# k k^T and k q^T of the delta rule as one three-part product, contiguous blocks from the transposes, and a remade table of issue

## The chip, the cores and the metric

One NeuronCore of a Trainium2 chip runs the whole program. The metric is the device time of one execution in microseconds (us), lower is better. In the profile PE is TensorE's matrix multiply and PEld its loading of weights, DVE is VectorE, ACT ScalarE, POOL GpSimd, and SP the engine that issues most DMAs.

## The reference

The model is an encoder of two layers over 512 positions of width 1024. Each layer projects its normalized input into three branches, gMLP, retention and a gated delta rule (here GDN), merges them with gates, and adds the result to its input. The change lies in the delta rule, which runs in both directions over chunks of 64 positions:

```python
def gdn_direction(q, k, v, beta, g):
    ...
    decay = jnp.exp(jnp.where(incl, gc[..., :, None] - gc[..., None, :], -jnp.inf))
    kb = kc * bc[..., None]
    lower = jnp.where(strict, jnp.einsum("nbhid,nbhjd->nbhij", kb, kc) * decay, 0.0)
    eye = jnp.eye(c, dtype=F32)
    rhs = jnp.concatenate([vc * bc[..., None], kb * jnp.exp(gc)[..., None]], axis=-1)
    sol = lax.linalg.triangular_solve(lower + eye, rhs, left_side=True, lower=True)
    u, w = sol[..., :GDN_HD], sol[..., GDN_HD:]

    def step(state, inp):
        qi, ki, ui, wi, gi, di = inp
        v_new = ui - jnp.einsum("bhcd,bhde->bhce", wi, state)
        scores = jnp.einsum("bhqd,bhkd->bhqk", qi, ki) * di
        out = (jnp.einsum("bhcd,bhde->bhce", qi * jnp.exp(gi)[..., None], state)
               + jnp.einsum("bhqk,bhke->bhqe", scores, v_new))
        ...
```

So per head and chunk k k^T and k q^T are needed, then the inverse of a lower triangular matrix.

## The kernel before

**Dense products.** All large products go through `mm3` (L279 to L283): each operand is split into a high part of type fp32r and the rest, and three products (high by high, high by low, low by high) add up in PSUM, each 128 rows, 128 columns of weights and 512 moving columns. The weights come by DMA from SP; ACT casts the high part (`hi`, L273) and DVE subtracts (`lo`, L274). PE runs such products through nearly the whole program, and DVE's L274 feeds it.

**The delta rule.** `gdn_pair(pi)` (L686) does two heads, `m` = 0 and 1; there are two pairs per layer, four in the program. It uses chunks of 128 positions, four per head. Its steps:

- L698 to L715: the dense products for k, q and v (`dpg`), a short convolution and SiLU on DVE and ACT, which give `kT` and `qT` (L684), and transposes on PE (`ptgg`, L706).
- L741 to L747: per head four products k k^T (`kkg`, L743) and four k q^T (`qkg`, L746) of 128x128 in plain fp32, each kind in a PSUM bank of its own out of the two of tag `gd`. PE takes a plain fp32 product as two records in the trace.
- L748 to L765: the decay factors `ef`, `eb`, `el` (L752, L754), and the products with them: `sl` (L757, L759) from k k^T, `pf` (L763) and `pb` (L765) from k q^T.
- L774 to L793: the inverse. DVE transposes blocks of 32x32 out of `sl` into `zn` (L774), runs 31 elimination steps over all blocks at once (L787, L789, result in `zv`), and transposes `zv` in two ways, into `ov` (L792, in the place of `zn`) and `ou` (L793). In both results the index of the matrix stands innermost, so one 32x32 block is read at a stride of 32 elements.
- L796 to L807: the blocks are joined. `px` (L799) has 32 products with `ov` as the moving operand, `xs` takes the result times -1 (L801 on ACT, L802 on DVE), and `py` (L806) has 32 products with `ou` as weights; all have 32 columns. The two halves `b` use the lower and the upper 64 rows.
- L809 to L865: copies into `sec` and `sl` (L816 to L818), two larger joins of the same kind with 64 columns (`pw`, L834; `pz`, L841 and L844), and scaling.
- L878 to L927: four steps of the scan in each direction.

**What sets the order.** At the end `in_order` (L139) ties the instructions of every engine into the order of the table `ORDER` (L26), a list of jumps and run lengths per engine: between the small steps of the delta rule PE has dense products of other branches. In pair 0 these are the gates and outputs of the retention branch (`merge(1, ...)`, tiles `pg` and `pb`), in pair 1 the gMLP branch and `merge(0, ...)`. An engine works its own list in order, and waits where an operand is not ready.

Of the kernel before, what the change touches and what calls it, by code (L numbers as in the profile page):

```python
# [8 lines left out]
F32 = mybir.dt.float32  # L9
# [6 lines left out]
P = 128  # L16
# [37 lines left out]
        427+8 -431+2 429+6 -435+2 544+4 -115 114+4 -118+110 8+5 43+4 -47+7 40+4 -44+36 8+480""",  # L54
    'DVE': """
# [102 lines left out]
def kernel(  # L158
# [215 lines left out]
    def layer(l, hT, rv_first=None, gate=None):  # L374
# [311 lines left out]
        def gdn_pair(pi):  # L686
# [48 lines left out]
            for m in range(2):  # L735
                h = 2 * pi + m

                def v4(t):
                    return t[:, m, :].rearrange("p (c d) -> p c d", c=4)

                pkk, pqk = p_gd(f"kk{nm}{m}"), p_gd(f"qk{nm}{m}")  # L741
                for c in range(4):
                    nc.tensor.matmul(pkk[:, c * P:(c + 1) * P], v4(kT)[:, c, :], v4(kT)[:, c, :],  # L743
                                          start=True, stop=True)
# [410 lines left out]
```

## Time and profile before

| | before |
|---|---|
| median of three runs | 1179.82 us (1179.53 to 1181.17) |
| the profiled execution's own time | 1181.15 us |
| its span in the profile | 1179.4 us |
| granted TensorE clock, mean | 0.998 |
| PE busy in the span | 1168.3 us, 99% |
| DVE busy | 808.2 us, 69% |
| ACT busy | 505.2 us, 43% |
| POOL busy | 259.8 us, 22% |

A busy PE in this table is one that has work in its pipeline, with ends that are modelled; what one product takes of PE's time is read as the distance from its start to the next one's start. The share of DVE is a mean: in the stretches of the delta rule it is far higher than 69%. Rows of the groups give the line, engine, operation, tiles, shape and count, then the total busy us and the mean ns of one, then the idle time ahead of it.

### The profile page before, as it was taken

The numbers are of one execution on the slowest core, as the hardware profiler recorded it, in microseconds if no ns is written. First come the engines' busy times: TensorE is split into PE (matmuls) and PEld (weight loads), VectorE is DVE, ScalarE is ACT, GpSimd is POOL, SyncE is SP. The second block draws the span as 40 slices with busy tenths as digits, with TensorE's granted clock in tenths as the row PEclk, the third lists the DMA queues.
The fourth block names the chain that finished last, engine by engine and source line by source line (L and its number), as shares of the span: only waits on it lengthen the run. The fifth ranks groups of instructions, "written<-read, shape, count | busy, mean of one in ns | idle before, by whom it ended". The sixth has DMA issues, their size and how long they took to land.

```text
span 1179.4 us, 17088 instructions
## 1 busy us (share of the span) xinstructions
PE 1168.3 (99%) x6390; PEld 973.4 (83%) x6390; DVE 808.2 (69%) x1626; ACT 505.2 (43%) x912; POOL 259.8 (22%) x244
## 2 busy tenths in 40 slices
PE   9999999999999999999999999999999999999997
PEld 6888788888888888888878887888888888888885
DVE  4478679967799875444444877898677997644433
ACT  5453453336554433433354435524375434234333
POOL 4154300013022222211223531000220221311122
PEclk9999999999999999999999999999999999999999
DMA  6321232313322214234533213232132232132343
GB/s 227 96 58 54 78 121 90 90 51 111 90 72 91 89 39 124 90 108 144 170 99 108 72 55 108 90 89 83 49 108 85 72 108 72 58 105 90 98 152 107
DMA packets 97131, 112.04 MB, mean 95 GB/s; under 512 B 6772, under 2 KB 81814, under 8 KB 97048
## 3 DMA queue, kind: packets, MB, share of 16 engines
q1 hardware_dynamic: 87188, 96.55, 26.9%
q10 hardware_dynamic: 9860, 14.40, 3.8%
q8 instruction: 50, 0.82, 0.3%
q14 instruction: 33, 0.27, 0.1%
HBM read 106.71 MB, written 4.23 MB: 94 GB/s over the span
## 4 chain that ended last, share of the span: by engine, by line
PE 97%; DVE 1%; DMA 1%; POOL 1%; ACT 0%; issue 0%; SPq 0%; ACTq 0%; POOLq 0%
PE pg L281 7%; PE pg L282 7%; PE pg L283 7%; PE pb L282 4%; PE dpg L282 4%; PE dpg L281 4%; PE pb L283 4%; PE pb L281 4%; PE dpg L283 4%; PE rp L282 2%; PE rp L281 2%; PE rp L283 2%; PE wo L282 2%; PE wo L283 2%; PE wo L281 2%; PE gv L282 1%
## 5 line engine op out<-in xcount | busy, mean ns | idle before, releaser
L274 DVE TENSOR_TENSOR lo<-raw,hi 128x512 fp32r<-128x512 f32 x340 | 253.3, 749 | 195.6 <-ACT hi L273 192.5
L273 ACT CAST hi<-raw 128x512 fp32r<-128x512 f32 x348 | 215.9, 623 | 392.1 <-PE pg L282 122.6
L281 PE MATMUL pg<-hh,hi 128*128 128x512 f32 x384 | 150.9, 393 | 0.0
L282 PE MATMUL pg<-hl,hi 128*128 128x512 f32 x384 | 150.3, 391 | 0.0
L283 PE MATMUL pg<-hh,lo 128*128 128x512 f32 x384 | 150.3, 391 | 0.0
L281 PEld LDWEIGHTS pg<-hh,hi 128*128 128x128 f32 x384 | 72.1, 188 | 14.9
L282 PEld LDWEIGHTS pg<-hl,hi 128*128 128x128 f32 x384 | 72.2, 188 | 14.4
L283 PEld LDWEIGHTS pg<-hh,lo 128*128 128x128 f32 x384 | 72.2, 188 | 14.3
L585 POOL TENSOR_TENSOR mg<-mg,gt 128x512 f32<-128x512 f32 x32 | 46.4, 1449 | 145.3 <-DVE gt L581 143.2
L281 PE MATMUL dpg<-hh,hi 128*128 128x512 f32 x192 | 76.3, 397 | 0.0
L283 PE MATMUL dpg<-hh,lo 128*128 128x512 f32 x192 | 75.4, 393 | 0.0
L282 PE MATMUL dpg<-hl,hi 128*128 128x512 f32 x192 | 75.3, 392 | 0.0
L281 PE MATMUL rp<-hh,hi 128*128 128x512 f32 x128 | 50.8, 397 | 0.0
L787 DVE TENSOR_TENSOR ztmpg<-zng,zvg 128x31 f32<-128x31 f32 (+15 forms) x124 | 48.4, 390 | 3.2
L282 PE MATMUL wo<-lo,mh 128*128 128x512 f32 x128 | 50.1, 391 | 0.4 <-DVE lo L274 0.4
L282 PE MATMUL rp<-hl,hi 128*128 128x512 f32 x128 | 50.3, 393 | 0.0
L283 PE MATMUL rp<-hh,lo 128*128 128x512 f32 x128 | 50.3, 393 | 0.0
L281 PE MATMUL wo<-hi,mh 128*128 128x512 f32 x128 | 50.0, 391 | 0.0
L283 PE MATMUL wo<-hi,ml 128*128 128x512 f32 x128 | 49.9, 390 | 0.0
L789 DVE TENSOR_TENSOR zvg<-zvg,ztmpg 128x31 f32<-128x31 f32 (+15 forms) x124 | 43.4, 350 | 3.1
L283 PEld LDWEIGHTS dpg<-hh,lo 128*128 128x128 f32 x192 | 36.1, 188 | 7.9
L281 PEld LDWEIGHTS dpg<-hh,hi 128*128 128x128 f32 x192 | 36.1, 188 | 7.2
(377 smaller groups left out, 2736.0 us busy)
## 6 DMA issues: line engine op xcount, KB each, us to landing
raw<-in_w_in_dram SPq DMA_DIRECT2D x86, 512.0 KB, 3.7
raw<-in_w_gate_dram SPq DMA_DIRECT2D x48, 512.0 KB, 3.7
raw<-in_w_branch_out_dram SPq DMA_DIRECT2D x24, 512.0 KB, 3.4
raw<-in_w_out_dram SPq DMA_DIRECT2D x16, 512.0 KB, 4.0
gbg<-gsc ACTq DMA_DIRECT2D x8, 512.0 KB, 3.8
xi<-in_x_dram SPq DMA_DIRECT2D x8, 256.0 KB, 6.6
xr<-in_x_dram ACTq DMA_DIRECT2D x8, 256.0 KB, 5.5
xd<-xr ACTq DMA_DIRECT2D x8, 256.0 KB, 5.7
```

Of the source, the lines that this page charges most:

```text
L273: nc.scalar.copy(hi, r)
L274: (eng or nc.vector).tensor_tensor(lo, r, hi.bitcast(F32), ALU.subtract)
L281: nc.tensor.matmul(o, lhs[0], rhs[0], start=start, stop=False)
L282: nc.tensor.matmul(o, lhs[0], rhs[1], start=False, stop=False)
L283: return nc.tensor.matmul(o, lhs[1], rhs[0], start=False, stop=stop)
L585: nc.gpsimd.tensor_tensor(mg[e][:, m, :], mg[e][:, m, :], ths[m], ALU.add)
L787: nc.vector.tensor_tensor(tv, zn[:, j + 1:32, j:j + 1].broadcast_to([P, n, w]), zv[:, j:j + 1, 0:w].broadcast_to([P, n, w]), ALU.mult)
L789: nc.vector.tensor_tensor(zv[:, j + 1:32, 0:w], zv[:, j + 1:32, 0:w], tv, ALU.subtract)
```

## The change

Three edits. First, k k^T and k q^T become one product per chunk: `kT` and `qT` are split like the dense operands into `kqh` (cast, ACT) and `kql` (subtraction, DVE), laid out chunk by chunk with k and q side by side, and `mm3` multiplies k of a chunk with the 256 columns of k and q. The result of chunks 0 and 1 lies in one PSUM bank, that of 2 and 3 in the other, k k^T and k q^T side by side. `pb` is then made in two halves. Second, both transposes of `zv` write with the matrix index outermost, so each 32x32 block is contiguous for `px`, `py` and the copies. Third, the table `ORDER` is remade.

```diff
 ORDER = {
     'PE': """
...
-                pkk, pqk = p_gd(f"kk{nm}{m}"), p_gd(f"qk{nm}{m}")
+
+                kqh, kql = (sp.tile([P, 4, 2, P], F32R, tag=f"kq{i}", bufs=1, name=f"kq{i}{nm}{m}") for i in range(2))
+                for i, t in enumerate((kT, qT)):
+                    nc.scalar.copy(kqh[:, :, i, :], v4(t))
+                    nc.vector.tensor_tensor(kql[:, :, i, :], v4(t), kqh[:, :, i, :].bitcast(F32), ALU.subtract)
+                pkq = [p_gd(f"kq{nm}{m}{i}").rearrange("p (c a d) -> p c a d", c=2, a=2) for i in range(2)]
                 for c in range(4):
-                    nc.tensor.matmul(pkk[:, c * P:(c + 1) * P], v4(kT)[:, c, :], v4(kT)[:, c, :],
-                                          start=True, stop=True)
-                for c in range(4):
-                    nc.tensor.matmul(pqk[:, c * P:(c + 1) * P], v4(kT)[:, c, :], v4(qT)[:, c, :],
-                                          start=True, stop=True)
+                    mm3(pkq[c // 2][:, c % 2].rearrange("p a d -> p (a d)"), (kqh[:, c, 0, :], kql[:, c, 0, :]),
+                        (kqh[:, c].rearrange("p a d -> p (a d)"), kql[:, c].rearrange("p a d -> p (a d)")), True, True)
...
-                nc.vector.tensor_tensor(pb[:, m, :], pqk, eb, ALU.mult)
+                for i in range(2):
+                    nc.vector.tensor_tensor(v4(pb)[:, 2 * i:2 * i + 2, :], pkq[i][:, :, 1],
+                                            eb.rearrange("p (c d) -> p c d", c=4)[:, 2 * i:2 * i + 2, :], ALU.mult)
...
-            ou = t_z4(f"ou{nm}").rearrange("p a b -> p (a b)").rearrange("p (f k) -> p f k", f=32)
-            ov = zn
-            nc.vector.transpose(ov, zv.rearrange("p i c -> p c i"))
-            nc.vector.transpose(ou, zv)
+            ou = t_z4(f"ou{nm}").rearrange("p a b -> p (a b)").rearrange("p (m k) -> p m k", m=32)
+            ov = zn.rearrange("p f k -> p (f k)").rearrange("p (m k) -> p m k", m=32)
+            nc.vector.transpose(ov.rearrange("p m i -> p i m"), zv.rearrange("p i c -> p c i"))
+            nc.vector.transpose(ou.rearrange("p m i -> p i m"), zv)
...
-                    nc.tensor.matmul(px3[b][0:32, m, :], sl[half[b], m, second[b]], ov[half[b], :, m],
+                    nc.tensor.matmul(px3[b][0:32, m, :], sl[half[b], m, second[b]], ov[half[b], m, :],
...
-                    nc.tensor.matmul(py3[b][0:32, m, :], ou[half[b], :, m], xs[half[b], m, :],
+                    nc.tensor.matmul(py3[b][0:32, m, :], ou[half[b], m, :], xs[half[b], m, :],
...
-                copy(sec[qs, :, q2], (ov[qs, :, 0:8] if q < 2 else ou[qs, :, 8:16]).rearrange("p i m -> p m i"))
-                copy(sl[qs, 8:16, qs], ov[qs, :, 8:16].rearrange("p i m -> p m i"))
-                copy(sl[qs, 0:8, qs], ou[qs, :, 0:8].rearrange("p i m -> p m i"))
+                copy(sec[qs, :, q2], ov[qs, 0:8, :] if q < 2 else ou[qs, 8:16, :])
+                copy(sl[qs, 8:16, qs], ov[qs, 8:16, :])
+                copy(sl[qs, 0:8, qs], ou[qs, 0:8, :])
```

The reads of `pkk` and `pqk` at L757 to L763 become reads of the halves of `pkq`, with the same shapes. Lines of the changed kernel are three to seven higher than those of before.

PE's order at the first head of the first pair, before: `kkg` stands right behind the transposes of k, among the dense products of q.

```order
L282 MATMUL dpg_1416<-hl_152,hi_1_1424 128x512
L706 MATMUL ptgg_1391<-cs,kTg_1307 128x128 x4
L743 MATMUL kkg_1630<-kTg_1307 128x128 x4
L283 MATMUL dpg_1416<-hh_151,lo_1_1425 128x512
L281 MATMUL dpg_1416<-hh_151,hi_1_1424 128x512
```

And after: the block stands behind the transposes of q, where `qkg` stood, with `kq0g` for `kqh` and `kq1g` for `kql`; of its twelve products these are ten.

```order
L284 MATMUL kqg_1636<-kq0g_1630 128x256
L284 MATMUL kqg_1637<-kq0g_1630 128x256
L284 MATMUL dpg_1517<-hh_151,hi_1_1524 128x512
L285 MATMUL dpg_1517<-hl_152,hi_1_1524 128x512
L286 MATMUL dpg_1517<-hh_151,lo_1_1525 128x512
L285 MATMUL kqg_1636<-kq1g_1631,kq0g_1630 128x256
L286 MATMUL kqg_1636<-kq0g_1630,kq1g_1631 128x256
L284 MATMUL kqg_1636<-kq0g_1630 128x256
L285 MATMUL kqg_1636<-kq1g_1631,kq0g_1630 128x256
L286 MATMUL kqg_1636<-kq0g_1630,kq1g_1631 128x256
L285 MATMUL kqg_1637<-kq1g_1631,kq0g_1630 128x256
L286 MATMUL kqg_1637<-kq0g_1630,kq1g_1631 128x256
```

k k^T has moved back by 55 dense products, to where both operands exist; the second head's block moves from behind the 569th dense product to two halves behind the 584th and the 593rd, counted from the program's start.

DVE's order behind the first `kT` of the first pair, before:

```order
L684 SCALAR_TENSOR_TENSOR kTg_1307<-ctg_1388,cvg_1384 128x512
L274 TENSOR_TENSOR lo_0_1521<-raw_1518,hi_0_1520 128x512
L713 TENSOR_REDUCE gss<-sgg_1396 128x4
L680 SCALAR_TENSOR_TENSOR cvg_1400<-dpg_1315,pc,cvg_1400 128x511
L681 SCALAR_TENSOR_TENSOR cvg_1400<-dpg_1315,pc,cvg_1400 128x511
```

And after, with the first of the new subtractions, which waits for ACT's cast into `kq0g`:

```order
L687 SCALAR_TENSOR_TENSOR kTg_1307<-ctg_1388,cvg_1384 128x512
L748 TENSOR_TENSOR kq1g_1631<-kTg_1307,kq0g_1630 128x4x128
L277 TENSOR_TENSOR lo_0_1521<-raw_1518,hi_0_1520 128x512
L716 TENSOR_REDUCE gss<-sgg_1396 128x4
L683 SCALAR_TENSOR_TENSOR cvg_1400<-dpg_1315,pc,cvg_1400 128x511
L684 SCALAR_TENSOR_TENSOR cvg_1400<-dpg_1315,pc,cvg_1400 128x511
```

The subtraction stands between `kT` and the low part of the next weights.

DVE's order around the two transposes of `zv` (first pair), before:

```order
L792 STREAM_TRANSPOSE zng_1712<-zvg_1713 128x1024
L274 TENSOR_TENSOR lo_1_2558<-raw_2551,hi_1_2557 128x512
L793 STREAM_TRANSPOSE oug_1788<-zvg_1713 128x1024
L274 TENSOR_TENSOR lo_0_2564<-raw_2561,hi_0_2563 128x512
L802 TENSOR_SCALAR xsg_1720<-pxg_1792 32x512
```

And after, where `xsg` is again the scaling of px's result that py reads:

```order
L277 TENSOR_TENSOR lo_1_2580<-raw_2573,hi_1_2579 128x512
L799 STREAM_TRANSPOSE zng_1734<-zvg_1735 128x32x32
L800 STREAM_TRANSPOSE oug_1810<-zvg_1735 128x32x32
L277 TENSOR_TENSOR lo_0_2586<-raw_2583,hi_0_2585 128x512
L584 SCALAR_TENSOR_TENSOR mg_2566<-gt_2526,pb_2540 128x512
L824 COPY slg_1629<-zng_1734 32x8x32
L809 TENSOR_SCALAR xsg_1742<-pxg_1814 32x512
```

The second transposition follows the first at once; a product of the merge and a copy now stand ahead of the scaling. On PE, px moves from behind the 808th to behind the 813th dense product of the program, and py from seven to eight dense products behind px.

More of the change, by code (lines that the diff above doesn't have):

```diff
@@ L27 @@
     'PE': """
[26 rows of a table removed]
-        427+8 -431+2 429+6 -435+2 544+4 -115 114+4 -118+110 8+5 43+4 -47+7 40+4 -44+36 8+480""",
[26 rows of a table added]
+        43+4 -47+7 40+4 -44+36 8+480""",
     'DVE': """
[1 row of a table removed]
[1 row of a table added]
         -121+3 16+2 -10+3 -7 6 -6 -2 38 -38 37+2 -35 34 -35+2 37 -35 -4 3 33 -32 -3 2 -3 2 5+3 27+2 -37+3 26 -22
[35 rows of a table removed]
-        -6 5 4+3 -7 1 4 -7 1 4+7 1+4 -5 4+5 3 -4 3 -4 3 -4 3+2""",
-    'Activation': """
[22 rows of a table removed]
-        -10+2 13+6 2 -3 2+3 -5 4+6 1 -2 3 -3+2 1 1 -2 1""",
-    'Pool': """
[4 rows of a table removed]
-        -2 1""",
[38 rows of a table added]
+        -4 3+2""",
+    'Activation': """
[23 rows of a table added]
+        -2 1""",
+    'Pool': """
[3 rows of a table added]
+        -5 4 20 1 -2 1 -21 1 18 1 -2 1+5 -24+7 17 -18+2 16 -17+3 14+18 1 -2 2 -2 2 -2 1""",
     'SP': """
@@ L756, in gdn_pair @@
                     cc = slice(c * P, (c + 1) * P)
-                    nc.vector.scalar_tensor_tensor(sl[:, m * 4 + c, :], pkk[:, cc], col(rb2, 0, h, c), ef[:, cc],
+                    nc.vector.scalar_tensor_tensor(sl[:, m * 4 + c, :], pkq[c // 2][:, c % 2, 0], col(rb2, 0, h, c), ef[:, cc],
                                                    ALU.mult, ALU.mult)
-                    nc.vector.scalar_tensor_tensor(sl[:, 8 + m * 4 + c, :], pkk[:, cc], col(rb2, 1, h, c),
+                    nc.vector.scalar_tensor_tensor(sl[:, 8 + m * 4 + c, :], pkq[c // 2][:, c % 2, 0], col(rb2, 1, h, c),
                                                    el[:, cc], ALU.mult, ALU.mult)
@@ L762, in gdn_pair @@
                     cc = slice(c * P, (c + 1) * P)
-                    nc.vector.scalar_tensor_tensor(v4(pf)[:, c, :], pqk[:, cc], col(rb2, 0, h, c), ef[:, cc],
+                    nc.vector.scalar_tensor_tensor(v4(pf)[:, c, :], pkq[c // 2][:, c % 2, 1], col(rb2, 0, h, c), ef[:, cc],
                                                    ALU.mult, ALU.mult)
-                nc.vector.tensor_tensor(pb[:, m, :], pqk, eb, ALU.mult)
+                for i in range(2):
+                    nc.vector.tensor_tensor(v4(pb)[:, 2 * i:2 * i + 2, :], pkq[i][:, :, 1],
+                                            eb.rearrange("p (c d) -> p c d", c=4)[:, 2 * i:2 * i + 2, :], ALU.mult)
             zn = t_z4(f"zn{nm}").rearrange("p a b -> p (a b)").rearrange("p (f k) -> p f k", f=32)
```

179 rows, old and new, of the table ORDER are left out of this document.

## Prediction

> **What bounds the kernel now.** First the page: the busy time of each engine and the shares of the chain that ended last.
>
> ```profile
> PE 1168.3 (99%) x6390; PEld 973.4 (83%) x6390; DVE 808.2 (69%) x1626; ACT 505.2 (43%) x912; POOL 259.8 (22%) x244
> ...
> PE 97%; DVE 1%; DMA 1%; POOL 1%; ACT 0%; issue 0%; SPq 0%; ACTq 0%; POOLq 0%
> ```
>
> TensorE (PE) is occupied for 99% of the span and 97% of the chain is its own work. So a change is worth what it takes off PE's queue, less the new waits that it makes PE take. Next the view of waits (us in total, times, longest), for the weight loads (PEld) that stand at the places that the change touches.
>
> ```profile
> PEld qkg L746 <- DVE pbg L765: 1.5, 4, 0.4
> ...
> PEld pxg L799 <- DVE lo L274: 0.7, 2, 0.4
> ```
>
> PE hardly waits there: 1.5 us over four places for k q^T of the second head of a pair, 0.7 us over two places for the small products px. The waits of before are therefore no reserve; the gain has to come from shorter PE work.
>
> **The change, part 1: k k^T and k q^T.** The timeline of PE shows one block of four fp32 products, and, further up, products whose moving side has only 16 columns.
>
> ```profile
> 140.54 0.29 PE L640 MATMUL pgc<-ga,cs 128*128 128x16 f32 x2
> 140.68 0.38 PE L641 MATMUL pgc<-ga,cs 128*128 128x16 f32 x2
> 140.90 0.39 PE L642 MATMUL pgc<-ga,cs 128*128 128x32 f32 x2
> 141.12 0.48 PE L281 MATMUL dpg<-hh,hi 128*128 128x512 f32 x1
> ...
> 147.04 1.06 PE L743 MATMUL kkg<-kTg 128*128 128x128 f32 x8
> 147.85 0.47 PE L283 MATMUL dpg<-hh,lo 128*128 128x512 f32 x1
> 148.17 0.39 PE L281 MATMUL dpg<-hh,hi 128*128 128x512 f32 x1
> 148.39 0.39 PE L282 MATMUL dpg<-hl,hi 128*128 128x512 f32 x1
> 148.62 0.40 PE L283 MATMUL dpg<-hh,lo 128*128 128x512 f32 x1
> ```
>
> Durations overlap, so I take the distance from start to start. Each fp32 product is two records. The eight records of a block take 147.85 - 147.04 = 0.81 us, and the dense product behind holds 0.32 us (to 148.17) where its neighbours hold about 0.23, so the block costs 0.90 us, 0.112 per record. The groups give the count.
>
> ```profile
> L746 PE MATMUL qkg<-qTg,kTg 128*128 128x128 f32 x64 | 8.9, 281 | 0.0
> ...
> L743 PE MATMUL kkg<-kTg 128*128 128x128 f32 x64 | 8.4, 275 | 0.0
> ```
>
> 128 records in 16 blocks go: 16 x 0.90 = 14.4 us. In their place come 12 products per head (four chunks, three parts), 96 in all, of 128x256 in fp32r, a width that the trace does not have. Bounds: the dense fp32r products of 512 columns stand 0.22 to 0.23 us apart, 0.227 in what follows; half of that is 0.114. From below, the products of 16 columns (140.68 to 141.12: four records in 0.44 us) still take 0.11 each, so loading 128 columns of weights sets a floor of 0.11. From above, a product of 256 columns could cost as much as one of 512: 0.227. The half is nearest, since the column count is what differs, and I add a little for a fixed part: 0.118. That gives 96 x 0.118 = 11.3 us. **Term: -3.1 us** (ends: 96 x 0.11 = 10.6, that is -3.8; 96 x 0.227 = 21.8, that is +7.4).
>
> **Part 2: px and py, contiguous instead of strided.** Per pair of heads these are 32 products each, 64 records, over 32 columns; in px the moving side, in py the weights are read at a stride of 32 elements. Timeline and groups:
>
> ```profile
> 234.96 1.99 PE L799 MATMUL pxg<-zng,slg 64*32 64x32 f32 x64
> 236.88 0.50 PE L282 MATMUL pb<-ylr,hi 128*128 128x512 f32 x1
> ...
> 238.70 2.01 PE L806 MATMUL pyg<-xsg,oug 64*32 64x32 f32 x64
> 240.64 0.50 PE L283 MATMUL pb<-yhr,lo 128*128 128x512 f32 x1
> ...
> 246.24 0.22 PE L841 MATMUL pzg<-slg,x2g 64*64 64x64 f32 x1
> 246.25 0.22 PE L834 MATMUL pwg<-slg 64*64 64x64 f32 x1
> ...
> 246.94 0.22 PE L841 MATMUL pzg<-slg,x2g 64*64 64x64 f32 x1
> ```
>
> ```profile
> L806 PEld LDWEIGHTS pyg<-xsg,oug 64*32 64x32 f32 x256 | 7.6, 147 | 1.5 <-issue 1.5
> ...
> L799 PEld LDWEIGHTS pxg<-zng,slg 64*32 64x32 f32 x256 | 7.4, 121 | 1.6 <-issue 0.9 <-DVE lo L274 0.7
> ...
> L834 PEld LDWEIGHTS pwg<-slg 64*64 64x64 f32 x64 | 4.3, 134 | 0.0
> ```
>
> A block of px holds PE for 236.88 - 234.96 = 1.92 us, one of py for 1.94. The records run in pairs, one on the lower and one on the upper half of the rows: 1.92 / 32 = 0.060 per pair with the edges of the block. The products pw and pz run in such pairs too, contiguous and twice as wide: from 246.24 to 246.94 twelve pairs of 64 columns, 0.058 each. So 32 strided columns cost what 64 contiguous ones cost. The loads say the same: a strided load of 32 columns takes 147 ns (py), a contiguous one of 64 columns 134, a contiguous one of 32 columns 121. By columns (0.112 for 128, 0.058 for 64, so 0.027 less for each halving that follows) a contiguous pair of 32 should take 0.031. I take a gain of 0.025 per pair: 32 pairs x 8 blocks x 0.025 = 6.4 us. **Term: -6.4 us** (ends: 0, if the pairs do not get shorter; 256 x 0.030 = -7.7).
>
> A rule of the Trainium skill speaks against this size: in "TensorE: Matmul & The Clock Gate", section "Wait — 56ns, not 53.3ns?", matmuls never start closer together than about 25 ns, however narrow they are. By it, 64 records would need 1.6 us, and the term would be an estimated 8 x 0.32 = -2.6 us. The trace contradicts it for records on different halves of the rows: 246.24 and 246.25 are 0.01 apart.
>
> **Part 3: what the other engines get.** Groups, then windows (start and end, length, and the busy us of PE, PEld, DVE, ACT and POOL with their instructions), then DVE's timeline around the transposition that frees px:
>
> ```profile
> L274 DVE TENSOR_TENSOR lo<-raw,hi 128x512 fp32r<-128x512 f32 x340 | 253.3, 749 | 195.6 <-ACT hi L273 192.5 <-PE pg L283 1.2
> ...
> L581 DVE SCALAR_TENSOR_TENSOR mg<-gt,pb 128x512 f32<-128x512 f32 x16 | 10.9, 683 | 0.2
> ...
> L902 DVE TENSOR_TENSOR xvg<-pxg,vsc 128x256 f32<-128x256 f32 x24 | 10.1, 420 | 7.0 <-ACT xvg L900 7.0
> ...
> L792 DVE STREAM_TRANSPOSE zng<-zvg 128x1024 f32<-128x1024 f32 x4 | 8.4, 2100 | 0.1
> ...
> L765 DVE TENSOR_TENSOR pbg<-qkg,ebg 128x512 f32<-128x512 f32 x8 | 5.5, 683 | 0.0
> ...
> L793 DVE STREAM_TRANSPOSE oug<-zvg 128x1024 f32<-128x1024 f32 x4 | 5.0, 1240 | 0.0
> ...
> L817 DVE COPY slg<-zng 32x256 f32<-32x256 f32 x8 | 3.0, 378 | 0.1
> ...
> L802 DVE TENSOR_SCALAR xsg<-pxg 32x512 f32<-32x512 f32 x4 | 2.7, 684 | 0.8 <-PE pxg L799 0.7
> ```
>
> ```profile
> 146.00:175.00 29.00, 29.00 (x148) 24.33 (x147) 22.03 (x47) 16.24 (x28) 2.90 (x1) 1.00 0.38 127
> 175.00:235.00 60.00, 59.94 (x277) 49.22 (x277) 58.06 (x138) 20.33 (x35) 1.04 (x2) 1.00 0.29 88
> 298.00:340.00 42.00, 42.00 (x221) 35.39 (x220) 33.57 (x80) 23.30 (x37) 2.91 (x1) 1.00 0.28 82
> 340.00:399.90 59.90, 59.90 (x274) 49.28 (x272) 57.64 (x105) 23.01 (x38) 15.27 (x12) 1.00 0.29 89
> ```
>
> ```profile
> 232.72 2.09 DVE L792 STREAM_TRANSPOSE zng<-zvg 128x1024 f32<-128x1024 f32 x1
> 234.74 0.65 DVE L274 TENSOR_TENSOR lo<-raw,hi 128x512 fp32r<-128x512 f32 x1
> 235.31 1.24 DVE L793 STREAM_TRANSPOSE oug<-zvg 128x1024 f32<-128x1024 f32 x1
> ```
>
> VectorE (DVE, the third busy time of a window) gets two subtractions per head, which are of the kind L274: 16 x 0.749 = 12.0 us. The product with eb is cut in two: 16 x 0.42 - 8 x 0.683 = +1.3 us. The two transposes now write strided. Before, L793 touches nothing strided (1.24 us) and L792 reads strided (2.10); a strided write is not in the trace. For each I bound the extra by 0 and by the 0.86 that the strided read costs, and take 0.86 for L793 and 0 for L792, which has a strided side already: 4 x 0.86 = +3.4 us (ends 0 and +6.9). ScalarE gets 16 casts, but is busy for at most 56% of any of the four windows. The copies become contiguous and can only get shorter; I count nothing.
>
> In all +16.7 us on DVE, 4.2 per pair of heads. The subtractions (3.0 per pair) have to lie ahead of the kq products, in the first window of a pair, where DVE has 29.00 - 22.03 = 7.0 us free (first pair) and 42.00 - 33.57 = 8.4 (second). That hides them. Without this cover they would slide into the second window, where only 1.9 and 2.3 us are free, and PE would wait for px: px starts at 234.96, right behind the transposition that ends at 232.72 + 2.09 = 234.81. The remade order gives some room: from the first transposition of k to px, PE has 366 dense products now against 359 in the first pair (7 x 0.227 = 1.6 us more, less 0.8 us that two heads of part 1 save), and 413 against 400 in the second (2.9 less 0.8). A second thing is late: both products of a head now lie in the same two banks, so the second head's can start only when all readers of the first are done; in the first pair the order puts them 15 and 24 dense products later than k k^T stood. Third, ahead of py: DVE now has, between the transposition that frees px and the scaling of px's result (L802 before), the second transposition, one subtraction, one product of the merge and one copy. By the rows above these are 1.24 to 2.10, 0.57 (235.31 - 234.74), 0.68 and up to 0.38, so 2.9 to 3.7 us, and 0.68 for the scaling: 3.6 to 4.4. In the first pair py stands eight dense products behind px, which with a px of 1.1 us is 1.1 + 1.8 = 2.9 and some 0.2 of edges. There PE should wait 0.5 to 1.3 us less what px itself stands behind its release; I take 0.6; in the second pair 16 products lie between, and nothing waits. I charge 2 x 0.6 and 0.3 for all the rest, the size of a few of today's waits. **Term: +1.5 us** (ends 0 and +4). SP's and POOL's queues pass no DMA over any other work by the edits themselves.
>
> **The sum.** -3.1 - 6.4 + 1.5 = -8.0 us. The profiled execution took 1181.15 us (span 1179.4 and 1.75 around it), so it would become 1173.15; it stands 1.33 above the median of the runs, 1179.82, so the median becomes **1171.8 us**.
>
> **Rivals.**
> - *The pairs do not get shorter.* px, py and the twice as wide pw with pz all take 0.058 to 0.060 per pair; that would also fit a limit on how fast four instructions (two loads, two products) are handed over. For it speaks that equality; against it that strided loads are measurably longer (147 against 121), and that starts 0.01 apart occur. Then only part 1 and the waits are left, -3.1 + 1.5 = -1.6: 1178.2. By the 25 ns of the page "TensorE: Matmul & The Clock Gate" of the Trainium skill it would be -3.1 - 2.6 + 1.5 = -4.2, an estimated 1175.6.
> - *A product of 256 columns costs as much as one of 512.* Part 1 becomes +7.4: 7.4 - 6.4 + 1.5 = +2.5, 1182.3. The trace has fp32r at 512 columns only, so nothing excludes it; that its rate is 0.44 ns per column, and that 16 columns cost 0.11, speaks against.
> - *DVE becomes the bound (slower).* If ScalarE's casts come late, DVE, which works in order, stands in front of the subtraction with the weights' low parts (L274) queued behind it, and the dense products wait for those. It decides once the added 4.2 us per pair no longer find the 7.0 and 8.4 us of the first windows, and so exceed the 1.9 and 2.3 of the second. In full: -9.5 + 16.7 = +7.2, 1187.0.
>
> **How the numbers follow.** Forecast 0.70, pairs unchanged 0.16, 256 columns slow 0.06, DVE bound 0.08. 0.2%, about what a measurement can tell from no change, is 2.4 us here, so faster means below 1177.5 and slower above 1182.2. The forecast is faster in 0.68 and within in 0.02; the first rival, just inside the bound, gives 0.06 faster and 0.10 same; the second, just at the other bound, 0.03 same and 0.03 slower; the third 0.02 same, where only part of it comes, and 0.06 slower. Together faster 0.74, same 0.17, slower 0.09. The range runs from the good ends without new waits (-3.8 - 7.7 = -11.5: 1168.3) to the first rival, 1178.2.
>
> **What would show it.** Start-to-start of the kq products near 0.118 us; blocks of px and py near 1.1 us instead of 1.92; PE's waits below 0.5 us at each kq and px and near 0.6 at the first pairs' py; DVE's busy time near 825 us; the two transposes near 2.1 us. A DVE that stands still for the casts in the first windows, a PE that waits microseconds for the transposition ahead of px, or blocks that still take 1.9 us would make it wrong.

## The result and the profile after

| | before | after |
|---|---|---|
| median of the runs on one chip | 1180.05 us (1179.53 to 1181.17, 4 runs) | 1170.91 us (1170.33 to 1171.98, 4 runs) |
| ratio after to before | | 0.9923, 95% interval 0.9908 to 0.9938 |
| span of the profiled execution | 1179.4 us | 1168.8 us |
| DVE busy | 808.2 us | 806.6 us |

The change takes 9.1 us off the time; 8.0 were forecast (1171.8 us). One execution of copies_act below ran at a granted clock of 0.754 and took 1444.51 us; it is left out, and a second run, copies_act_again, gives that experiment's profile.

First the page of the changed kernel: its busy times, and how the chain of work that ended last divides among the engines.

```profile
PE 1157.0 (99%) x6358; PEld 964.1 (82%) x6358; DVE 806.6 (69%) x1650; ACT 501.4 (43%) x924; POOL 262.0 (22%) x244
...
PE 96%; DVE 2%; POOL 1%; DMA 0%; ACT 0%; issue 0%; SPq 0%; POOLq 0%; DVEq 0%; ACTq 0%
```

PE is still the bound and has 11.3 us less to do, but DVE's share of the chain went from 1% to 2%: something waits for it now that did not wait before. The timeline of PE at the first head's products (start and duration in us, line, tiles, shape; where it stands, in brackets the idle time ahead and what ended it):

```profile
159.26 0.28 PE L285 MATMUL kqg<-kq1g,kq0g 128*128 128x256 f32 x1
...
160.45 0.40 PE L284 MATMUL dpg<-hh,hi 128*128 128x512 f32 x1
160.68 0.40 PE L285 MATMUL dpg<-hl,hi 128*128 128x512 f32 x1
```

Ten products from 159.26 to 160.45: 0.119 us each, and the dense product behind holds its usual 0.23 us (160.45 to 160.68), not the 0.32 that stood behind a block of plain fp32. Next PE around px and py, in the first pair and, in the last two rows, in the second:

```profile
233.87 1.20 PE L806 MATMUL pxg<-zng,slg 64*32 64x32 f32 x64 [0.28 <-DVE zng L799]
235.00 0.50 PE L284 MATMUL pb<-yhr,hi 128*128 128x512 f32 x1
...
237.10 0.24 PE L813 MATMUL pyg<-xsg,oug 64*32 64x32 f32 x2
237.62 1.20 PE L813 MATMUL pyg<-xsg,oug 64*32 64x32 f32 x62 [0.28 <-DVE xsg L809]
238.75 0.50 PE L286 MATMUL gv<-hi,hl 128*128 128x512 f32 x1
...
403.15 1.24 PE L813 MATMUL pyg<-xsg,oug 64*32 64x32 f32 x64
404.32 0.50 PE L285 MATMUL pg<-hl,hi 128*128 128x512 f32 x1
```

px takes 235.00 - 233.87 = 1.13 us (1.92 before), py in the second pair 404.32 - 403.15 = 1.17 (1.94 before). In the first pair py spans 1.65 us, for two records start at 237.10 and the rest only at 237.62: the upper half of the rows had to wait for DVE's scaling. Why, the timeline of DVE shows:

```profile
231.54 2.18 DVE L799 STREAM_TRANSPOSE zng<-zvg 128x1024 f32<-128x1024 f32 x1
233.62 1.95 DVE L800 STREAM_TRANSPOSE oug<-zvg 128x1024 f32<-128x1024 f32 x1
235.40 0.69 DVE L277 TENSOR_TENSOR lo<-raw,hi 128x512 fp32r<-128x512 f32 x1
236.00 0.68 DVE L584 SCALAR_TENSOR_TENSOR mg<-gt,pb 128x512 f32<-128x512 f32 x1
236.59 0.26 DVE L824 COPY slg<-zng 32x256 f32<-32x256 f32 x1
236.88 0.68 DVE L809 TENSOR_SCALAR xsg<-pxg 32x512 f32<-32x512 f32 x1
```

PE goes on from px at 235.00, and DVE's scaling of its result starts at 236.88; DVE works without a gap in between. Next, DVE's copies out of the second transposition, before and after (shortest, median and longest ns):

```profile
L818 DVE COPY slg<-oug x8: 362/366/1375, 240.1 to 984.7; 32x256 f32<-32x256 f32 x8
```

```profile
L825 DVE COPY slg<-oug x8: 273/282/285, 239.7 to 980.4; 32x256 f32<-32x256 f32 x8
```

And the groups of DVE after (busy us, mean ns):

```profile
L277 DVE TENSOR_TENSOR lo<-raw,hi 128x512 fp32r<-128x512 f32 x340 | 249.0, 737 | 189.5 <-ACT hi L276 184.4 <-PE rp L286 2.2 <-PE ptgg L709 0.3
...
L799 DVE STREAM_TRANSPOSE zng<-zvg 128x1024 f32<-128x1024 f32 x4 | 8.8, 2210 | 0.1
...
L800 DVE STREAM_TRANSPOSE oug<-zvg 128x1024 f32<-128x1024 f32 x4 | 8.1, 2019 | 0.0
...
L771 DVE TENSOR_TENSOR pbg<-kqg,ebg 128x256 f32<-128x256 f32 x16 | 6.6, 415 | 0.0
...
L748 DVE TENSOR_TENSOR kq1g<-kTg,kq0g 128x512 fp32r<-128x512 f32 x8 | 5.5, 690 | 2.5 <-ACT kq0g L747 2.5
...
L748 DVE TENSOR_TENSOR kq1g<-qTg,kq0g 128x512 fp32r<-128x512 f32 x8 | 5.5, 688 | 2.8 <-ACT kq0g L747 2.8
```

### The profile page after: what moved, and what is told of

Its sections match the earlier page's. It is cut to its first block, busy times and chain, and to the rows that moved or that the text cites. A ratio compares the mean times of both kernels' runs of the same rounds, so it can differ in the third digit from the quotient of the medians.

```text
span 1168.8 us, 17057 instructions
## 1 busy us (share of the span) xinstructions
PE 1157.0 (99%) x6358; PEld 964.1 (82%) x6358; DVE 806.6 (69%) x1650; ACT 501.4 (43%) x924; POOL 262.0 (22%) x244
## 4 chain that ended last, share of the span: by engine, by line
PE 96%; DVE 2%; POOL 1%; DMA 0%; ACT 0%; issue 0%; SPq 0%; POOLq 0%; DVEq 0%; ACTq 0%
PE pg L285 7%; PE pg L284 7%; PE pg L286 7%; PE dpg L284 4%; PE dpg L286 4%; PE dpg L285 4%; PE pb L286 4%; PE pb L284 4%; PE pb L285 4%; PE rp L285 2%; PE rp L284 2%; PE rp L286 2%; PE wo L285 2%; PE wo L286 2%; PE wo L284 2%; PE gv L286 1%
## 5 line engine op out<-in xcount | busy, mean ns | idle before, releaser
L277 DVE TENSOR_TENSOR lo<-raw,hi 128x512 fp32r<-128x512 f32 x340 | 249.0, 737 | 189.5 <-ACT hi L276 184.4
L796 DVE TENSOR_TENSOR zvg<-zvg,ztmpg 128x31 f32<-128x31 f32 (+15 forms) x124 | 47.2, 381 | 3.1
L794 DVE TENSOR_TENSOR ztmpg<-zng,zvg 128x31 f32<-128x31 f32 (+15 forms) x124 | 44.3, 358 | 2.7
```

What stands on the lines that cost most here:

```text
L277: (eng or nc.vector).tensor_tensor(lo, r, hi.bitcast(F32), ALU.subtract)
L794: nc.vector.tensor_tensor(tv, zn[:, j + 1:32, j:j + 1].broadcast_to([P, n, w]), zv[:, j:j + 1, 0:w].broadcast_to([P, n, w]), ALU.mult)
L796: nc.vector.tensor_tensor(zv[:, j + 1:32, 0:w], zv[:, j + 1:32, 0:w], tv, ALU.subtract)
```

## The experiments

Each was timed beside the kernel before on the same chip. The times are medians of four to seven runs; those marked * are one run.

| experiment | median, us | before beside it | difference |
|---|---|---|---|
| contig_only | 1176.98 | 1180.01 | -3.0 |
| kq_only | 1175.52 | 1180.01 | -4.5 |
| late_px | 1170.96 | 1180.01 | -9.1 |
| sub_twice | 1171.89 | 1180.01 | -8.1 |
| late_chain | 1172.19 | 1180.12 | -7.9 |
| table_pe | 1211.18 | 1180.12 | +31.1 |
| kq_128 * | 1170.27 | 1180.12 | -9.9 |
| serial * | 1176.29 | 1180.12 | -3.8 |
| copies_act | 1170.91 | 1180.39 | -9.5 |
| stride2 * | 1169.47 | 1180.39 | -10.9 |
| ou_stride2 | 1169.52 | 1179.93 | -10.4 |
| copies_act_again * | 1171.32 | 1179.93 | -8.6 |

### One part at a time

**contig_only** is the kernel before with the layout edits of the change's diff alone:

```diff
-            nc.vector.transpose(ov, zv.rearrange("p i c -> p c i"))
-            nc.vector.transpose(ou, zv)
+            nc.vector.transpose(ov.rearrange("p m i -> p i m"), zv.rearrange("p i c -> p c i"))
+            nc.vector.transpose(ou.rearrange("p m i -> p i m"), zv)
```

> The kernel before with the contiguous blocks alone (both transposes write with the matrix index outermost; px, py and the copies read accordingly), with its own table of issue. Theory of columns and stride: a block of px takes 1.13 us and one of py 1.17 instead of 1.92 and 1.94, as in the changed kernel, so 8 blocks give -6.2 us. The second transposition takes 2.0 instead of 1.24 us, and the table was not made for that: in the first pair of each layer the scaling ahead of py should end 0.9 us later while PE arrives 0.8 us sooner, so PE waits 0.7 us there, 1.5 us in all. Sum about -4.7 us against before, 1175.3. Rival, the blocks got shorter only together with the new table: blocks near 1.9 us and a time within 1 us of before.

Measured: 1176.98 us, ratio 0.9973 (0.9963 to 0.9984). PE's timeline in the first pair:

```profile
234.83 1.20 PE L799 MATMUL pxg<-zng,slg 64*32 64x32 f32 x64 [0.15 <-DVE zng L792]
...
238.28 1.38 PE L806 MATMUL pyg<-xsg,oug 64*32 64x32 f32 x64 [0.42 <-ACT xsg L801]
...
242.81 1.14 PE L834 MATMUL pwg<-secg,slg 64*64 64x64 f32 x16 [0.43 <-ACT secg L824]
```

The blocks are as short with the old table (px 1.13 from start to start in every pair, py 1.13 to 1.15 in the second pairs, where it does not wait), so the table is not what shortened them. The wait at py came as expected, but its start waits for ACT's scaling: that stands behind a copy on ACT for which ACT idles 1.45 us until the second transposition ends. The wait at pw the expectation did not have. Before, pw starts 0.32 us behind the start of the dense product ahead of it; here it is 0.82 and 0.79 us in the first pairs and 0.50 and 0.47 in the second, so 1.3 us more in all, of the 1.7 by which the gain fell short. What PE saves in px and py, the work on DVE and ACT between px and pw does not follow.

**kq_only** is the changed kernel with the layout put back:

> The changed kernel with the layout of the blocks put back (px and py read at a stride of 32 elements again); the three-part product and the remade table stay. Theory: blocks of px and py take 1.92 and 1.94 us again, +6.2 us; the 1.0 us that PE waits inside the first pairs' py in the changed kernel goes, since the second transposition is 0.8 us shorter and PE arrives 0.8 us later. Sum +5.2, about 1176.1, that is -3.9 against before: -3.1 for the products and up to -1 that neither part explains. Rival, the remade table and not the products gave the rest: then the twelve products per head take as long as the eight blocks of records that they replace (14.4 us), and PE's gain lies in waits elsewhere.

Measured: 1175.52 us, ratio 0.9961 (0.9949 to 0.9974). PE's timeline in the first pair:

```profile
237.71 2.01 PE L813 MATMUL pyg<-xsg,oug 64*32 64x32 f32 x64
239.65 0.50 PE L286 MATMUL gv<-hi,hl 128*128 128x512 f32 x1
```

The blocks are at 1.91 and 1.94 us again, and no wait stands at py. -4.5 us is more than the -3.1 forecast for the products. The products themselves are worth what was forecast: added from start to start over the trace, the 128 records of before hold 13.4 us and the 16 dense products behind them 16 x (0.313 - 0.227) = 1.4 us above their own; the 96 products hold 11.8 us (96 x 0.119, and 0.1 us more at four places) and nothing behind them. That is -2.9. By this difference the remade table saves about another 1.6 us outside the products; no run has the whole new table without them, so the size is not shown directly. With contig_only the sum is -7.5, and both together give -9.1: the new table also leaves less waiting. Against before, PE's delays at px, py and pw grow by 2.9 us in contig_only and by 1.6 in the changed kernel.

Where the table saves, PE's timeline in the retention branch shows (pss, pwr, pk and pyr are its small products), here before:

```profile
103.95 1.06 PE L464 MATMUL pss<-rqT,rkT 128*128 128x128 f32 x8
104.77 0.47 PE L282 MATMUL rz<-hl,hi 128*128 128x512 f32 x1
105.08 0.40 PE L283 MATMUL rz<-hh,lo 128*128 128x512 f32 x1
...
106.41 0.94 PE L479 MATMUL pk<-vt,rkf 128*128 128x128 f32 x6
107.22 0.94 PE L479 MATMUL pk<-vt,rkb 128*128 128x128 f32 x6
...
108.66 0.39 PE L282 MATMUL rz<-hl,hi 128*128 128x512 f32 x1
```

And in table_pe, with PE's new order:

```profile
104.17 1.06 PE L464 MATMUL pss<-rqT,rkT 128*128 128x128 f32 x8
...
106.37 0.83 PE L479 MATMUL pk<-vt,rkf 128*128 128x128 f32 x6
107.04 0.83 PE L479 MATMUL pk<-vt,rkb 128*128 128x128 f32 x6
...
107.94 0.40 PE L283 MATMUL rz<-hh,lo 128*128 128x512 f32 x1
```

Before, 108.66 - 103.95 = 4.71 us, and within it stand three dense products, two behind pss and one behind pyr (just ahead of 108.66); with the new order 107.94 - 104.17 = 3.77 with one (just ahead of 107.94). 4.71 - 2 x 0.227 - 3.77 = 0.49 us less per layer for the same small products: the first pk, for one, took 0.81 us from start to start before (106.41 to 107.22), now 0.67. The changed kernel's trace has the same 3.77 us.

**table_pe** was meant to show the table's share alone: the kernel before with PE's new order, and nothing else new.

> The kernel before with the new order of PE alone (the plain fp32 products k k^T and k q^T of a head stand where the three-part products stand in the new table; the other engines keep their old order). Theory: beside the products and the blocks, the new table itself saves about 1.5 us, because on PE it puts small blocks of the retention branch (po and pss with pwr, pyr and pk) behind one another and so saves places where dense and small products change, 1.0 us in the two profiles, and 0.5 us at pm; so 1178.0 to 1178.8, and no more with the old order elsewhere, whose waits may take part of it back. Rival, the table saves nothing by itself and the products gain more than 3.1 us: time within 0.5 us of before or above it.

It does not show that: 1211.18 us. PE's waits (us in all, times, longest), of which these are the two largest, say why.

```profile
PE pm L975 <- DVE szgz L367: 6.6, 2, 3.3
PE pyr L519 <- POOL oc L511: 5.7, 2, 2.9
```

PE reaches its work before DVE and POOL, in their old order, have made it ready. One engine's row of the table alone made the kernel slower here. What the run does show is the 0.49 us per layer above: it comes with PE's order and without either edit. The remaining 0.6 of the table's 1.6 us is not settled.

### The products: columns or weights

**kq_128** narrows the products to k k^T; k q^T is left out:

```diff
-                    mm3(pkq[c // 2][:, c % 2].rearrange("p a d -> p (a d)"), (kqh[:, c, 0, :], kql[:, c, 0, :]),
-                        (kqh[:, c].rearrange("p a d -> p (a d)"), kql[:, c].rearrange("p a d -> p (a d)")), True, True)
+                    mm3(pkq[c // 2][:, c % 2, 0], (kqh[:, c, 0, :], kql[:, c, 0, :]),
+                        (kqh[:, c, 0, :], kql[:, c, 0, :]), True, True)
```

> The changed kernel with the three-part products 128 columns wide: k q^T is left out, and pf and pb read k k^T in its place. Theory of the prediction, loading 128 columns of weights sets a floor of 0.11 us per product: the products follow each other at 0.11 instead of 0.12 us, so 96 x 0.01 = -1 us. Rival, columns alone set the time (0.44 ns each): 0.06 us per product, 96 x 0.06 = -5.8 us.

PE's timeline:

```profile
159.18 0.22 PE L285 MATMUL kqg<-kq1g,kq0g 128*128 128x128 f32 x1
...
160.24 0.44 PE L284 MATMUL dpg<-hh,hi 128*128 128x512 f32 x1
160.52 0.40 PE L285 MATMUL dpg<-hl,hi 128*128 128x512 f32 x1
```

Ten products in 1.06 us, 0.106 each against 0.119: half the columns save a tenth. So the floor near 0.11 us holds at 128 columns too, and the dense product behind takes 0.28 us instead of 0.23, so part of even that is given back. That loading the weights is what sets the floor fits, but no run varied it by itself. For the change it means that k k^T and k q^T side by side in one product pay: with the weights of k, k q^T adds 0.013 us per product.

### The blocks: halves, and how wide a stride

**serial** orders px and py by half of the rows:

```diff
-            for m in range(16):
-                for b in range(2):
+            for b in range(2):
+                for m in range(16):
```

> The changed kernel with px and py each ordered by half: all 32 records on the lower 64 rows, then all on the upper, instead of one of each in turn. Theory: records overlap because neighbours use different halves of the rows, and one record on its own takes about 0.031 us; a block then takes 64 x 0.031 = 2.0 us instead of 1.13 and 1.17, and the time grows by 8 x 0.8 = 6 us less some waits that this hides. Rival, records follow at 0.018 us whatever rows they use: blocks stay at 1.1 to 1.2 us. The 25 ns of the Trainium skill's page TensorE: Matmul & The Clock Gate would make it an estimated 1.6 us.

```profile
234.12 2.08 PE L806 MATMUL pxg<-zng,slg 64*32 64x32 f32 x64 [0.26 <-DVE zng L799]
236.13 0.50 PE L284 MATMUL pb<-yhr,hi 128*128 128x512 f32 x1
```

236.13 - 234.12 = 2.01 us, 2.04 for py, and 1176.29 us in all, as the first theory had it: 2.01 / 64 = 0.031 us per record when neighbours use the same rows, 1.13 / 64 = 0.018 when they alternate.

**stride2** reads the blocks at a stride of 2 elements, two matrix indices innermost:

```diff
-            ov = zn.rearrange("p f k -> p (f k)").rearrange("p (m k) -> p m k", m=32)
-            nc.vector.transpose(ov.rearrange("p m i -> p i m"), zv.rearrange("p i c -> p c i"))
+            ov = zn.rearrange("p f k -> p (f k)").rearrange("p (a i b) -> p a i b", a=16, b=2)
+            nc.vector.transpose(ov.rearrange("p a i b -> p i a b"), zv.rearrange("p i c -> p c i"))
...
-                                     ov[half[b], m, :],
+                                     ov[half[b], m // 2, :, m % 2],
...
-                copy(sec[qs, :, q2], ov[qs, 0:8, :] if q < 2 else ou[qs, 8:16, :])
+                copy(sec[qs, :, q2].rearrange("p (a b) i -> p a i b", b=2), ov[qs, 0:4] if q < 2 else ou[qs, 4:8])
```

and the same for `ou` and the copies into `sl`.

> The changed kernel with the blocks of px and py read at a stride of 2 elements instead of 1 (two indices of the matrix innermost in both transposed results; the copies read accordingly). Theory, any stride costs the double: blocks of 1.9 us as at a stride of 32, time near 1176. Rival, only wide strides cost: blocks stay at 1.13 to 1.2 us, time near 1171.

The rival was right, and more came of it: px and py stay at 1.13 to 1.18 us, the second transposition is fast again, and the one run took 1169.47 us. The copies out of these tiles, though, are slow again, 0.41 us on DVE against 0.28: as written here they read their source in its order in memory, and write neighbours 64 elements (`sec`) or 128 (`sl`) apart. **ou_stride2** therefore keeps the first result contiguous and puts only the second at a stride of 2.

> The changed kernel with the second transposition's result alone at a stride of 2 elements (py's weights and the copies out of it read at that stride; the first transposition's result stays contiguous). Theory from the look at stride 2: PE reads a stride of 2 at no extra cost (blocks of 1.13), the second transposition takes 1.2 instead of 2.0 us, so in the first pairs the scaling ahead of py comes 0.8 us sooner, PE's waits inside py (0.48 and 0.49 us) go, and only a part of them comes back at pw: 1169.5, about 1.4 us below the changed kernel, as that look gave with both results at stride 2; the copies out of the first result stay at 0.28 us, so perhaps 0.3 less. Rival, the single time of that look was a good execution and no more: 1170.6 or above.

PE, and the groups of DVE:

```profile
236.82 1.20 PE L813 MATMUL pyg<-xsg,oug 64*32 64x32 f32 x64
237.96 0.50 PE L286 MATMUL gv<-hi,hl 128*128 128x512 f32 x1
...
240.23 1.14 PE L841 MATMUL pwg<-secg,slg 64*64 64x64 f32 x16
```

```profile
L800 DVE STREAM_TRANSPOSE oug<-zvg 128x1024 f32<-128x1024 f32 x4 | 4.9, 1222 | 0.0
```

py takes 1.14 us with no wait, and pw has none either. 1169.52 us (1168.93 to 1169.89), ratio to before 0.9913 (0.9896 to 0.9929). All four runs lie below all four of the changed kernel (1170.33 to 1171.98); the two were not timed side by side, but the kernel before took 1179.93 us beside this one and 1180.05 beside that. With the one run of stride2 (1169.47) it is the fastest version found here, 1.4 us below the changed kernel.

### What sets the pace from px to pw

**late_px** moves entries of the table in the first pair of each layer, on PE, DVE and ACT. On DVE:

```diff
 L277 TENSOR_TENSOR lo_0_2586<-raw_2583,hi_0_2585 128x512
+L809 TENSOR_SCALAR xsg_1742<-pxg_1814 32x512
 L584 SCALAR_TENSOR_TENSOR mg_2566<-gt_2526,pb_2540 128x512
-L824 COPY slg_1629<-zng_1734 32x8x32
-L809 TENSOR_SCALAR xsg_1742<-pxg_1814 32x512
-L824 COPY slg_1629<-zng_1734 32x8x32
+L824 COPY slg_1629<-zng_1734 32x8x32 x2
```

> The changed kernel with a few entries of the table moved in the first pair of each layer: px and py stand two dense products later on PE, and the scaling of px's result stands ahead of the merge's product and a copy on DVE, and ahead of two copies on ACT. Theory: the waits at px (0.44 and 0.22 us before its start, beyond 0.09 of edge) and inside py (0.48 and 0.49 us) go: -1.0 to -1.4 us, 1169.7; PE then has no stop beside either block. Rival, DVE as a whole sets the pace there: the waits come back a little later (at pw, or at dense products that wait for the merge), and the time stays within 0.3 us.

1170.96 us: the rival. PE's timeline:

```profile
241.43 1.14 PE L841 MATMUL pwg<-secg,slg 64*64 64x64 f32 x16 [0.71 <-ACT secg L831]
```

The waits at px and py are gone, and stand at pw, which starts 1.21 and 1.14 us behind the product ahead of it (0.36 in the changed kernel). **late_chain** takes the next step on DVE:

> The kernel with px and py two dense products later and the scaling first (late_px), and beside it, in the first pair of each layer, the transpositions of py's result (L828) on DVE ahead of the second product of the merge, a copy, one subtraction for the dense products and two further copies that stood ahead of them. Theory: late_px gained nothing because the same work of DVE that PE no longer waits for at px and py made it wait 0.98 and 0.91 us at pw, for the copies of ACT behind these transpositions; taking 1.9 us of other work out of DVE's way there frees pw, so -1.7 us against late_px, 1169.2. Rival, DVE has no time left in these windows at all: the delayed subtraction makes dense products wait, or the wait moves on to pz, and the time stays within 0.3 us of 1170.9.

1172.19 us (five runs from 1171.64 to 1174.55), worse than late_px (1170.80 to 1171.16) by 1.2. PE, then DVE:

```profile
241.17 0.49 PE L285 MATMUL gv<-lo,hh 128*128 128x512 f32 x1 [1.14 <-DVE lo L277]
```

```profile
240.43 0.69 DVE L277 TENSOR_TENSOR lo<-raw,hi 128x512 fp32r<-128x512 f32 x1
```

pw no longer waits, but now a dense product waits 1.14 us for the subtraction that was put back. In this stretch DVE is full (its timeline has no gap above 0.04 us from 233.7 to 241.6): a reordering only chooses who waits. **copies_act** starts from late_px and takes work off DVE instead:

```diff
-                copy(sec[qs, :, q2], ov[qs, 0:8, :] if q < 2 else ou[qs, 8:16, :])
-                copy(sl[qs, 8:16, qs], ov[qs, 8:16, :])
+                nc.scalar.copy(sec[qs, :, q2], ov[qs, 0:8, :] if q < 2 else ou[qs, 8:16, :])
+                nc.scalar.copy(sl[qs, 8:16, qs], ov[qs, 8:16, :])
```

> The kernel with px and py two dense products later and the scaling first (late_px), and the four copies per pair out of the first transposition's result that DVE makes (two of L823, two of L824) made by ACT, which idles there. Theory: in the first pair of each layer DVE has no time left from px to pw, so work that is only put later on DVE (late_chain) comes back as a wait, while work that leaves DVE does not: 4 x 0.28 = 1.1 us less ahead of the transpositions of py's result, so PE's waits of 0.98 and 0.91 us at pw fall to 0.1 or less: -1.7 us against late_px, 1169.2. Rival, another resource is behind the wait at pw (ACT's own copies, which get 1.6 us longer per pair): waits at pw of 0.9 us or more stay, 1171 or above.

> The kernel with four copies per pair on ACT instead of DVE, once more, since the profile of its first run was of an execution at a granted clock of 0.754 and shows no waits of a normal one; its timed executions gained nothing. Theory, DVE was not alone behind the wait at pw: the wait stands there still, now behind ACT, whose copies end later. Rival, pw waits no more, and the same 1 us stands somewhere behind it (pz, the scan), where the profile should show a new wait on PE.

No gain again, but for a reason of the experiment's own. PE, in the first pair and in the second, then DVE and ACT in the second:

```profile
240.81 1.14 PE L841 MATMUL pwg<-secg,slg 64*64 64x64 f32 x16
...
403.48 0.22 PE L813 MATMUL pyg<-xsg,oug 64*32 64x32 f32 x2 [0.54 <-DVE oug L800]
```

```profile
400.20 1.19 DVE L277 TENSOR_TENSOR lo<-raw,hi 128x512 fp32r<-128x512 f32 x1 [1.37 <-ACT hi L276]
```

```profile
399.12 0.41 ACT L824 COPY slg<-zng 32x256 f32<-32x256 f32 x1 [1.17 <-PE pxg L806]
```

In the first pair pw starts without a wait, as the theory said. But the copies were moved in both pairs, and in the second one of them stands on ACT ahead of a cast that DVE's subtraction needs. That copy writes over what px reads, and ACT idled 1.17 us until px was through; DVE stood still for 1.37 us, the second transposition came later, and PE waited for it at py. Neither expectation had that. Moving the copies in the first pairs alone was not tried.

**sub_twice** asks the opposite question, whether the subtractions of the change are hidden:

```diff
-                    nc.vector.tensor_tensor(kql[:, :, i, :], v4(t), kqh[:, :, i, :].bitcast(F32), ALU.subtract)
+                    for _ in range(2):
+                        nc.vector.tensor_tensor(kql[:, :, i, :], v4(t), kqh[:, :, i, :].bitcast(F32), ALU.subtract)
```

> The changed kernel with each of the 16 new subtractions done twice (the second writes the same values), which puts 16 x 0.69 = 11.0 us more on DVE, 2.8 us per pair of heads, right where the new ones stand. Theory, DVE's idle time in the first window of a pair covers them (4.5 us free in the first pair and 7.3 in the second with the change): time within 1 us of the changed kernel, 1171 to 1172, px's start no later than 0.3 us. Rival, DVE is the bound through the pair: px starts up to 2.8 us later in each pair, and the time grows by 5 to 11 us.

1171.89 us (1171.59 to 1172.05; the changed kernel 1170.33 to 1171.98): +1.0 for 11 us of DVE's time. They are hidden but for about 1 us. PE's waits in its trace have one, at a product of the gMLP branch, that the changed kernel's do not:

```profile
PE pm L984 <- DVE cvg L685: 0.6, 2, 0.3
```

## Why the prediction was right

- **What bounds.** PE's own work, as read: its busy time fell by 11.3 us, the time by 9.1.
- **Part 1, -3.1 us.** -2.9 by the distances above: 0.119 us per product against 0.118 taken. The floor of 0.11 was nearly right too (0.106 in kq_128). The sum counted the 0.09 us that a dense product holds longer behind the old blocks, and nothing of the kind behind the new products, without giving a reason. That it holds 0.23 us there was luck, 1.4 us of it.
- **Part 2, -6.4 us.** 4 x (1.92 - 1.13) + 4 x (1.94 - 1.17) = 6.2. The gain of 0.025 us per pair was the right size. The reason was right in one half: a pair costs less because its block is not read at a stride of 32, as contig_only shows; but "contiguous" is more than it needs, a stride of 2 does as well. The first rival, a limit on handing over instructions, falls with the blocks of 1.13 us. The page "TensorE: Matmul & The Clock Gate" of the Trainium skill (section "Wait — 56ns, not 53.3ns?") has matmuls never closer than about 25 ns. Here 64 records start within 1.13 us, 18 ns apart, when they alternate between halves of the rows, so its minimum does not hold for these; with neighbours on the same half they stand 31 ns apart (serial), which agrees with it.
- **Part 3, the load on DVE.** Subtractions 11.0 us (12.0 forecast, at a mean of 749 ns that holds the long ones below; the median before is 0.69 us too), halves of pb 6.6 - 5.5 = +1.1 (1.3), transpositions 8.8 + 8.1 - 8.4 - 5.0 = +3.5 (3.4, and in the transposition where it was expected: 1240 to 2019 ns). But DVE's busy time fell by 1.6 us instead of rising by 16.7. Busy time counts overlaps once; the durations of its instructions add up to 2.7 us more than before, where these three parts add 15.6. One part of the difference is the layout of the copies, which I counted at nothing: DVE's 24 went from 0.37 or 0.38 us to 0.28, 2.2 us in all. Another is long records, 6 us. Two of the eight copies of L818 took about 1.38 us before, and still do in contig_only (and in table_pe) but not in kq_only or after, so the layout is not what ended them; the new orders of DVE and POOL or the products are. The subtraction for the dense products (253.3 us, now 249.0) has such records too: 29 of its 340 took over 0.8 us before and in contig_only, 23 in kq_only and after, and 20 in table_pe, where PE's order alone is new. Each of these long records overlaps an operation of POOL. About 4 us of the difference stay open.
- **The waits, +1.5 us.** Over the two layers PE's delays at px and py grew by about 1.3 us, from start to start against before: 0.23 ahead of px, 0.07 ahead of py, and 0.48 and 0.49 inside py (1.65 and 1.67 us against 1.17). That is the place (the first pairs' py, 0.6 each) and the cause (the second transposition, the product of the merge and a copy ahead of the scaling) of the forecast. Its size rested on the cover being short there, and the experiments show how short: from px to pw DVE has no time to give. At pw come 0.34 us more, most of it in the second pairs, where the forecast named no wait.
- **What was missing.** The remade table was weighed only as room for px. It also saved about 1.6 us elsewhere, 2 x 0.49 of that at pk and its neighbours; 0.6 has no place yet. That is the term the sum lacked: with 1.6 for the waits, pw's among them, -2.9 - 6.2 + 1.6 - 1.6 = -9.1. The whole forecast was 1.1 us short.
- **The rivals.** Columns of 256 as dear as 512: no, 0.119 against 0.227. DVE as the bound: not over a pair (sub_twice), but between px and pw, for 1 to 2 us in the program, yes.

## What to carry to other kernels

When a block on the bounding engine gets shorter, look at the engines that feed it from there to the next block: the old order gave back about half of a gain of 6.2 us as waits (contig_only), and moving entries within a full engine's order only moved the wait, from px and py to pw or to a dense product. Work taken off that engine ended the wait at pw in the first pairs, but made a new one where the engine that got it stood in front of something else (copies_act). Between two engines that want opposite layouts, try a small stride before choosing a side: two elements side by side kept both TensorE's reads and VectorE's transposition fast.

## What was not expected of the hardware

- TensorE's records of 32 columns cost the same at a stride of 1 and of 2 elements (1.13 to 1.18 us for 64), and 1.92 at a stride of 32. Strides between were not tried. The page "SBUF — State Buffer" of the Trainium skill (section "Door 1: The DMA port swizzle (why `[64,N]` ≈ `[32,N]`)") gives a reason that fits: the memory has lines of 16 bytes, and two accesses in a row to one line are enough for full speed, which two fp32 numbers at a stride of 2 are and two at a stride of 32 are not.
- VectorE's 128x1024 transposition with a contiguous source (the second) takes 1.22 us when it writes pairs of neighbouring elements, 1.24 contiguously, and 2.02 when each element lands 32 away. The first, which reads at a stride of 32, takes 2.11, 2.10 and 2.21 in these three layouts: two strided sides cost little more than one. Copies of 32x256 take 0.28 us on VectorE and 0.40 on ScalarE when both sides are contiguous, 0.37 to 0.39 and 0.63 to 0.65 when they read at a stride of 32 (before, kq_only), and 0.41 and 0.64 to 0.66 when they write neighbours 64 or 128 apart (stride2). No run has a copy whose elements lie at a stride of 2.
- Products of 256 columns in fp32r leave no extra time behind them, those of 128 columns 0.05 us, plain fp32 products of 128 columns 0.09.
- The same instruction on VectorE can take far longer beside one on GpSimd: a copy of 32x256 1.38 us instead of 0.28 (contig_only, beside a 1.29 us multiplication on POOL). All 29 long subtractions of before overlap one on POOL; so do 50 of its 311 short ones, so an overlap alone does not decide it.
